# Attention probabilities scaled before their transposes on GpSimd, in place of scaling the product with the values

## The chip, the cores and the metric

The kernel runs on one core of a Trainium2 chip. The metric is the device time of one execution in microseconds (us); a lower one is better. The engines are named as the profile names them: PE is TensorE's matmul unit and PEld its weight load, DVE is VectorE, ACT is ScalarE, POOL is GpSimd, SP is SyncE, which issues the DMAs here.

## The reference

Two decoder layers over 512 tokens of width 1024. Each layer projects the normalised stream to two groups of attention heads: eight heads with a sliding window of 128 keys, two key heads and a learned sink, and eight heads with one key head, whose keys are chosen per query by an indexer (the best 128). Both groups go through one output projection; after it come a layer norm, a SwiGLU network of width 2816 with a gated input embedding, and another layer norm. What bears on the change is the softmax and the product with the values:

```python
# window group: the sink adds to the sum alone
m = jnp.maximum(s.max(-1, keepdims=True), sink)
pr = jnp.exp(s - m)
denom = pr.sum(-1, keepdims=True) + jnp.exp(sink - m)
o = jnp.einsum('bnhgqk,bnkhd->bnqhgd', (pr / denom).astype(v.dtype), vv)
...
# sparse group, over the chosen keys
pr = jax.nn.softmax(s, axis=-1)
o = jnp.einsum('bqhgj,bqjhd->bqhgd', pr.astype(v.dtype), vs)
```

All is float32.

## The kernel before

Tokens lie in four tiles of 128. Large products are made in three passes of a rounded format: each operand is split into a high half (a cast, on ACT) and a low half (what the cast lost, a subtract), and `mm3` (lines 325 to 327) multiplies high by high, high by low and low by high. The stream's own halves, turned so that features lie on partitions, are `fh` and `fl`; weight halves are in `wsp`, made by lines 278 (ACT) and 279 (POOL) of `w_split`, and by 256 and 257 for the down projection.

Attention is cut into 32 units, 16 a layer: a unit is one group of four heads on one tile of queries. Eight units of the window group come first ("a", with 128 keys for the first tile and 256 for the others), then eight of the sparse group ("b", with 128, 256, 384 and 512 keys, tile by tile). The sparse group computes all keys up to the query's tile and adds a mask that the top-k left in `work`.

A unit has two generators. `scores` multiplies queries by keys (L684), adds the mask and takes the row's extreme on DVE (L688), takes the exponential in place on ACT with the row's sum as a by-product (L692), adds the sink's share for the window group (L695 on POOL, L696 on ACT, L697 on POOL), and takes the reciprocal of the four sums on DVE (L698). The exponentials `es` are 128 queries by n keys for each head, not yet divided. L700 on POOL spreads the four reciprocals over `rb`, 128 x 256, 64 equal columns for each head.

`values` turns the exponentials on PE, 128 keys at a time, four heads to a bank (L721), copies them to SBUF on ACT (L723) and multiplies them with the values (`pv`, L715); two heads lie above each other on the 128 partitions of the product, so a product is 128 x 256. `rb` is turned too (L732) and copied to SBUF (L735), so that the reciprocals lie as the product does. DVE multiplies product and reciprocals (L740), ACT casts the result to its high half (L747), and POOL subtracts for the low half (L748). For the window group the halves go to a tile of their own, `ma`; for the sparse group straight into `fh` and `fl`.

The order of the work is written by Python generators that `Order.run` takes in turn by the cost that each yields. In a layer three streams run side by side: `attention`, in which the scores of a unit run beside the values of the unit two before it (`AHEAD` = 2); `rest`, which projects the sparse group's queries, waits for all units of the window group and then makes that group's half of the output projection; and `topk`, 16 rounds of two DVE operations for each of three tiles (L659, L660, and L662 at the end). From the order written down and from its own estimate of durations, the framework then lays out each engine's queue when the program is made; each engine works through its queue in that order. Scratch tiles `t2k` come from a pool of 12, PSUM banks from a pool of 8, shared by all.

Of the kernel before, what the change touches and what calls it, by code (L numbers as in the profile page):

```python
# [10 lines left out]
F32 = mybir.dt.float32  # L11
# [4 lines left out]
OP = mybir.AluOpType  # L16
# [80 lines left out]
def hybrid_kernel(ctx: ExitStack, tc: tile.TileContext, x, p, positions, ln_in_g, ln_in_b, w_in,  # L97
# [3 lines left out]
    PE, V, A, G, SP = nc.tensor, nc.vector, nc.scalar, nc.gpsimd, nc.sync  # L101
# [6 lines left out]
    small = ctx.enter_context(tc.tile_pool(name="small", bufs=4))  # L108
# [4 lines left out]
    def bank(tag, bufs, dt=F32):  # L113
        return psum.tile([128, 512], dt, name="bank", tag="bank", bufs=8)

    def acc():
        return bank("acc", 4)

    def slot(dt=F32R):
        return slots.tile([128, 512], dt, name="slot", tag="slot")  # L120

    def t2k(dt=F32):
        return tmp.tile([128, 512], dt, name="t2k", tag="t2k")

    def sm(n, name):
        return small.tile([128, n], F32, name=name, tag=name)
# [20 lines left out]
    idf = const.tile([128, 128], F32, name="idf")  # L147
# [200 lines left out]
    def tok(t):  # L348
        return slice(t * 128, (t + 1) * 128)
# [198 lines left out]
    for l in range(L):  # L548
# [84 lines left out]
        def wait(*keys):  # L633
            while not all(k in ready for k in keys):
                yield None
# [30 lines left out]
        def scores(kind, t, g, st):  # L666
            if kind == "a":
                k0, nk, c = max(0, t - 1) * 128, (256 if t else 128), g
                mask = win if t else win[:, 128:]
                yield from wait((kind, t, g), *[("k", b) for b in range(max(2, t + 1))])  # L670
            else:
                k0, nk, c = 0, (t + 1) * 128, 2
                yield from wait((kind, t, g), *[("k", b) for b in range(max(2, t + 1))], *[("s", t)] * (t > 0))
                mask = work[t] if t else causal[:, S - 128:]
            nn = max(nk, 256)
            per = 512 // nn
            ng, sums = sm(4, "ng"), sm(4, "sums")
            es = []
            for j in range(4):
                if j % per == 0:  # L680
                    ps, e = bank("sc", 2), t2k()
                o = j % per * nn
                for s in range(2):
                    PE.matmul(ps[:, o:o + nn], qT[kind, t, g][:, j * 128:(j + 1) * 128], kT[c, s][:, k0:k0 + nn],  # L684
                              start=(s == 0), stop=(s == 1))
                es.append(e[:, o:o + nk])
                far = nsink[:, l, 4 * g + j:4 * g + j + 1] if kind == "a" else 3e38
                V.tensor_tensor_reduce(es[j], ps[:, o:o + nk], mask, -HD ** -0.5, far, op0=OP.add, op1=OP.min,  # L688
                                       accum_out=ng[:, j:j + 1])
                yield 0.44 * nn / 512  # L690
            for j in range(4):
                A.activation(es[j], es[j], AF.Exp, bias=ng[:, j:j + 1], scale=-1.0, accum_out=sums[:, j:j + 1])  # L692
            if kind == "a":
                ek = sm(4, "ek")
                G.tensor_tensor(ek, sink[:, l, 4 * g:4 * g + 4], ng, OP.add)  # L695
                A.activation(ek, ek, AF.Exp)  # L696
                G.tensor_tensor(sums, sums, ek, OP.add)  # L697
            V.reciprocal(sums, sums)  # L698
            rb = small.tile([128, 256], F32, name="rb", tag="rb", bufs=3)
            G.tensor_copy(rb.rearrange("p (j d) -> p j d", j=4), sums[:, :, None].to_broadcast([128, 4, 64]))  # L700
            st.extend([es, rb, k0 // 128, nk // 128])

        def values(kind, t, g, st):

            es, rb, b0, nb = st
            c = g if kind == "a" else 2
            o = acc()[:, :256].rearrange("p (a n) -> p a n", a=2)
            pts = {}
            lag, cost = LAG[kind], 0.45
            if kind == "b":  # L710
                yield from wait("x read")

            def pv(b):
                for u in range(2):
                    PE.matmul(o[u * 64:(u + 1) * 64], vt[b0 + b][:, c * 64:(c + 1) * 64], pts[b][:, u],  # L715
                              start=b == 0, stop=b == nb - 1)

            for b in range(nb):
                ps = bank("tp", 2)
                for j in range(4):  # L720
                    PE.transpose(ps[:, j * 128:(j + 1) * 128], es[j][:, b * 128:(b + 1) * 128], idf)  # L721
                pt = t2k()
                A.copy(pt, ps)  # L723
                pts[b] = pt.rearrange("p (a u n) -> p u a n", a=2, u=2)
                yield 0.44
                if b >= lag:
                    pv(b - lag)
                    yield cost

            pr = bank("tp", 2)  # L730
            for a in range(2):
                PE.transpose(pr[:, a * 128:(a + 1) * 128], rb[:, a * 128:(a + 1) * 128], idf)  # L732
            tt = t2k()
            rr, of = (tt[:, i * 256:(i + 1) * 256].rearrange("p (a n) -> p a n", a=2) for i in range(2))
            A.copy(rr, pr[:, :256].rearrange("p (a n) -> p a n", a=2))  # L735
            yield 0.44
            for b in range(max(0, nb - lag), nb):
                pv(b)
                yield cost
            V.tensor_tensor(of, o, rr, OP.mult)  # L740
            if kind == "a":
                m = ma[t, g] = slot().rearrange("p (s a n) -> p s a n", s=2, a=2)
                hi, lo = m[:, 0], m[:, 1]
            else:
                k = 4 + 2 * g
                hi, lo = fh[:, k:k + 2, tok(t)], fl[:, k:k + 2, tok(t)]
            A.copy(hi, of)  # L747
            G.tensor_tensor(lo, of, hi, OP.subtract)  # L748
            ready.add(("m" + kind, t, g))

        units = [("a", t, g) for g in range(2) for t in range(NT)] + [("b", t, g) for t in range(NT) for g in range(2)]
# [1 line left out]
        def attention():  # L753

            st = {}
            for i in range(len(units) + AHEAD):
                gs = []
                if i in FILL:
                    yield 0.0, FILL[i]
                if i < len(units):  # L760
                    st[i] = []
                    gs.append(scores(*units[i], st[i]))
                if i >= AHEAD:
                    gs.append(values(*units[i - AHEAD], st.pop(i - AHEAD)))
                while gs:
                    none = True
                    for g in list(gs):
                        try:
                            c = next(g)
                        except StopIteration:  # L770
                            gs.remove(g)
                            none = False
                            continue
                        if c is not None:
                            none = False
                            yield c
                    if none:
                        yield None
# [186 lines left out]
        for gi, fs in enumerate(GROUPS):  # L965
            hs = []
            for f in fs:
# [7 lines left out]
                if gi == 1 and f == fs[0]:  # L975
                    pT = {}
                    for k in range(2):
                        ps = bank("tp", 2)
                        for t in range(NT):
                            o = t % 2 * 256 + k * 128  # L980
# [12 lines left out]
            for h in range(2):  # L993
                ps = [acc() for _ in range(NT)]
                n = len(hs)
# [13 lines left out]
        for b in TAIL:  # L1009
            for h in range(2):  # L1010
# [18 lines left out]
                for i, t in enumerate(b):  # L1029
                    a = t2k()  # L1030
# [37 lines left out]
```

## Time and profile before

| | |
|---|---|
| median of 3 runs | 1251.89 us (1251.59 to 1252.14) |
| the profiled execution | 1251.81 us, its span 1249.7 us |
| granted TensorE clock, mean | 0.998 |
| attention, layer 1 | 98 to 206 us of the span, about |
| attention, layer 2 | 702 to 816 us of the span, about |

How rows are read. A window's row gives its length and then, for each engine, the time in which it was busy and the number of instructions. A group's row has line, engine, operation, the tile written and the tiles read, the shapes and the count, then the busy time and the mean of one in ns, then the idle time of the engine before these instructions and what ended it. A row of one line's durations has minimum, median and maximum in ns, then the first and last start in us. A row of the timeline has start and duration in us, and in brackets the idle time before it. A row of the waits has who waited for whom, us in total, times, and the longest. The chain is the work that ended last, followed backwards; its row gives lines' shares of the window asked for.

### The profile page before, as it was taken

What the parts mean: (1) busy time and instruction counts of PE and PEld (TensorE: products, weight loads), DVE (VectorE), ACT (ScalarE), POOL (GpSimd) and SP (SyncE); (2) the same over time, 40 slices, a digit from 0 to 9 for tenths busy, and PEclk for the clock granted to TensorE, in tenths of its full rate; (3) what the DMA queues carried; (4) which work ended last, traced back from release to release, by engine and by line L of the source; (5) the groups of instructions that cost most, each with busy time, mean ns of one, the idle gap of its engine ahead of it and who ended that gap; (6) DMA issues with size and microseconds to landing.
All of it is one profiled execution on the core that took longest, in us unless ns stands there. A gap on an engine that the chain in (4) does not pass through costs nothing.

```text
span 1249.7 us, 18006 instructions
## 1 busy us (share of the span) xinstructions
PE 1225.9 (98%) x6552; PEld 1029.9 (82%) x6552; DVE 765.2 (61%) x1678; ACT 576.4 (46%) x1193; POOL 682.9 (55%) x555
## 2 busy tenths in 40 slices
PE   7999999999999999999999999999999999999996
PEld 5998777988888888888899987689888888888885
DVE  7699954682727272726677998286555555555365
ACT  6577763442434343433337787534343333333331
POOL 6885532566566666663169754234757575757400
PEclk9999999999999999999999999999999999999999
DMA  5232311333232323034033203114323333321321
GB/s 177 78 92 85 95 42 35 119 118 118 85 118 84 118 85 118 18 118 140 2 89 114 101 21 117 52 54 149 99 87 105 97 105 99 103 83 52 101 84 50
DMA packets 89264, 112.74 MB, mean 90 GB/s; under 512 B 5460, under 2 KB 66132, under 8 KB 89176
## 3 DMA queue, kind: packets, MB, share of 16 engines
q1 hardware_dynamic: 88504, 111.58, 28.5%
q8 instruction: 51, 0.84, 0.3%
q14 instruction: 37, 0.30, 0.1%
q10 hardware_dynamic: 672, 0.03, 0.0%
HBM read 109.49 MB, written 2.10 MB: 89 GB/s over the span
## 4 chain that ended last, share of the span: by engine, by line
PE 82%; POOL 5%; DVE 3%; issue 3%; ACT 3%; DMA 3%; SPq 0%; DVEq 0%; ACTq 0%; POOLq 0%
PE bank L325 24%; PE bank L326 24%; PE bank L327 24%; PE bank L715 3%; PE bank L684 3%; PE bank L721 2%; POOL wsp L279 2%; DMA wst<-in_w_pg_dram 2%; POOL wsp L257 1%; PE bank L523 1%; PE bank L438 1%; PE bank L732 1%; ACT wsp L278 1%; DVE slot L273 1%; POOL slot L517 1%
## 5 line engine op out<-in xcount | busy, mean ns | idle before, releaser
L279 POOL TENSOR_TENSOR wsp<-wst,wsp 128x1024 fp32r<-128x1024 f32 (+2 forms) x148 | 351.3, 2389 | 244.4 <-ACT wsp L278 240.8
L326 PE MATMUL bank<-fl,wsp 128*128 128x512 f32 (+1 forms) x768 | 284.8, 372 | 0.4 <-DVE fl L441 0.4
L325 PE MATMUL bank<-fh,wsp 128*128 128x512 f32 (+1 forms) x768 | 283.6, 372 | 1.0 <-ACT fh L440 1.0
L327 PE MATMUL bank<-fh,wsp 128*128 128x512 f32 (+1 forms) x768 | 283.1, 371 | 0.0
L278 ACT CAST wsp<-wst 128x1024 fp32r<-128x1024 f32 (+2 forms) x148 | 151.6, 1033 | 166.4 <-PE bank L327 126.2
L325 PE MATMUL bank<-wsp,fh 128*128 128x256 f32 (+3 forms) x512 | 165.2, 326 | 3.6 <-DVE work L648 2.0
L874 DVE TENSOR_TENSOR t2k<-bank,t2k 128x512 f32<-128x512 f32 x44 | 30.4, 692 | 222.0 <-PE bank L327 222.0
L326 PEld LDWEIGHTS bank<-fl,wsp 128*128 128x128 f32 x768 | 144.6, 188 | 25.7 <-DVE fl L441 0.9
L325 PEld LDWEIGHTS bank<-fh,wsp 128*128 128x128 f32 x768 | 143.6, 188 | 26.8 <-ACT fh L440 1.9
L327 PEld LDWEIGHTS bank<-fh,wsp 128*128 128x128 f32 x768 | 144.6, 188 | 24.9
L327 PE MATMUL bank<-wsp,fl 128*128 128x256 f32 (+3 forms) x512 | 163.7, 322 | 1.4 <-DVE fl L441 0.8
L326 PE MATMUL bank<-wsp,fh 128*128 128x256 f32 (+3 forms) x512 | 164.7, 322 | 0.0
L257 POOL TENSOR_TENSOR wsp<-slot,wsp 128x512 fp32r<-128x512 f32 x100 | 141.6, 1442 | 29.0 <-ACT wsp L256 29.0
L325 PE MATMUL bank<-wsp,slot 128*128 128x512 f32 x392 | 153.8, 392 | 0.0
L326 PE MATMUL bank<-wsp,slot 128*128 128x512 f32 x392 | 152.7, 390 | 0.0
L327 PE MATMUL bank<-wsp,slot 128*128 128x512 f32 x392 | 148.4, 390 | 0.0
L790 DVE TENSOR_TENSOR x<-bank,x 128x512 f32<-128x512 f32 x140 | 91.5, 684 | 88.5 <-PE bank L327 88.5
L904 ACT CAST slot<-t2k 128x256 fp32r<-128x256 f32 (+1 forms) x104 | 49.8, 497 | 144.1 <-DVE t2k L874 102.5
L257 POOL TENSOR_TENSOR wsp<-t2k,wsp 128x512 fp32r<-128x512 f32 x40 | 57.5, 1448 | 92.4 <-ACT wsp L256 92.4
L325 PEld LDWEIGHTS bank<-wsp,fh 128*128 128x128 f32 x512 | 97.6, 191 | 11.9 <-ACT fh L440 2.4
L327 PEld LDWEIGHTS bank<-wsp,fl 128*128 128x128 f32 x512 | 97.5, 191 | 7.9 <-DVE fl L441 1.1
L326 PEld LDWEIGHTS bank<-wsp,fh 128*128 128x128 f32 x512 | 98.0, 191 | 6.5 <-issue 1.2
(152 smaller groups left out, 2004.6 us busy)
## 6 DMA issues: line engine op xcount, KB each, us to landing
wst<-in_w_gu_dram SPq DMA_DIRECT2D x88, 512.0 KB, 3.5
slot<-in_w_down_dram SPq DMA_DIRECT2D x80, 256.0 KB, 2.8
wst<-in_w_in_dram SPq DMA_DIRECT2D x16, 512.0 KB, 3.6
wst<-in_w_o_dram SPq DMA_DIRECT2D x16, 512.0 KB, 3.8
wst<-in_w_pg_dram SPq DMA_DIRECT2D x16, 512.0 KB, 4.2
wst<-in_w_in_dram SPq DMA_DIRECT2D x8, 256.0 KB, 2.7
lng<-in_ln_g_dram SPq DMA_DIRECT2D x4, 512.0 KB, 4.8
lnb<-in_ln_b_dram SPq DMA_DIRECT2D x4, 512.0 KB, 5.5
```

The costliest lines, as they stand in the source:

```text
L257: G.tensor_tensor(w[:, 1, j], src[j], w[:, 0, j], OP.subtract)
L278: A.copy(w[:, 0, :a * n], st[:, :a * n])
L279: G.tensor_tensor(w[:, 1, :a * n], st[:, :a * n], w[:, 0, :a * n], OP.subtract)
L325: PE.matmul(o, sh, mh, start=start, stop=False, skip_group_check=again)
L326: PE.matmul(o, sh, ml, start=False, stop=False, skip_group_check=again)
L327: PE.matmul(o, sl, mh, start=False, stop=stop, skip_group_check=again)
L684: PE.matmul(ps[:, o:o + nn], qT[kind, t, g][:, j * 128:(j + 1) * 128], kT[c, s][:, k0:k0 + nn], start=(s == 0), stop=(s == 1))
L715: PE.matmul(o[u * 64:(u + 1) * 64], vt[b0 + b][:, c * 64:(c + 1) * 64], pts[b][:, u], start=b == 0, stop=b == nb - 1)
L721: PE.transpose(ps[:, j * 128:(j + 1) * 128], es[j][:, b * 128:(b + 1) * 128], idf)
L790: V.tensor_tensor(xt[t][:, c], ps, xt[t][:, c], OP.add)
L874: V.tensor_tensor(a, ps[1, f], a, OP.mult)
L904: A.copy(h[0], src)
```

## The change

`scores` no longer makes `rb`. Instead POOL multiplies each head's exponentials in place by the head's reciprocal, four instructions of 128 x n, each with a column of 128 numbers as the factor. `values` transposes these probabilities, so the product with the values needs no factor afterwards: the two transposes of `rb`, their PSUM bank, the copy, the scratch tile and the multiplication on DVE go. ACT casts the high half straight from the product in PSUM, and the low half's subtract moves from POOL to DVE, also reading PSUM. The step in the middle of `values` yields a cost of 0.22 instead of 0.44.

```diff
             V.reciprocal(sums, sums)
-            rb = small.tile([128, 256], F32, name="rb", tag="rb", bufs=3)
-            G.tensor_copy(rb.rearrange("p (j d) -> p j d", j=4), sums[:, :, None].to_broadcast([128, 4, 64]))
-            st.extend([es, rb, k0 // 128, nk // 128])
+            for j in range(4):
+                G.tensor_scalar(es[j], es[j], sums[:, j:j + 1], 1.0, op0=OP.mult, op1=OP.mult)
+            st.extend([es, k0 // 128, nk // 128])
 
         def values(kind, t, g, st):
 
-            es, rb, b0, nb = st
+            es, b0, nb = st
...
-            pr = bank("tp", 2)
-            for a in range(2):
-                PE.transpose(pr[:, a * 128:(a + 1) * 128], rb[:, a * 128:(a + 1) * 128], idf)
-            tt = t2k()
-            rr, of = (tt[:, i * 256:(i + 1) * 256].rearrange("p (a n) -> p a n", a=2) for i in range(2))
-            A.copy(rr, pr[:, :256].rearrange("p (a n) -> p a n", a=2))
-            yield 0.44
+            yield 0.22
             for b in range(max(0, nb - lag), nb):
                 pv(b)
                 yield cost
-            V.tensor_tensor(of, o, rr, OP.mult)
...
-            A.copy(hi, of)
-            G.tensor_tensor(lo, of, hi, OP.subtract)
+            A.copy(hi, o)
+            V.tensor_tensor(lo, o, hi, OP.subtract)
             ready.add(("m" + kind, t, g))
```

## The prediction

> **What bounds the kernel now.** I read the page's busy shares first, then the busy time of the engines in the four stretches in which attention runs, then the chain that ended last inside these stretches.
>
> ```profile
> span 1249.7 us, 18006 instructions
> PE 1225.9 (98%) x6552; PEld 1029.9 (82%) x6552; DVE 765.2 (61%) x1678; ACT 576.4 (46%) x1193; POOL 682.9 (55%) x555
> ```
> ```profile
> core 0: us, PE busy (x) PEld busy (x) DVE busy (x) ACT busy (x) POOL busy (x), PEclk, DMA share, GB/s
> 85.40:165.00 79.60, 78.81 (x589) 66.89 (x589) 73.47 (x245) 61.52 (x183) 45.61 (x66) 1.00 0.26 80
> 165.00:206.00 41.00, 41.00 (x238) 28.41 (x238) 13.52 (x40) 23.11 (x57) 13.47 (x14) 1.00 0.17 52
> 698.00:760.00 62.00, 61.08 (x476) 52.53 (x475) 59.31 (x196) 47.29 (x149) 38.31 (x59) 1.00 0.27 90
> 760.00:816.00 56.00, 55.75 (x327) 40.16 (x326) 27.41 (x86) 34.90 (x89) 18.11 (x19) 1.00 0.17 53
> ```
>
> In each layer attention has a first part (sliding-window units and the first sparse ones, rows one and three) and a second (sparse units over 384 and 512 keys, rows two and four). PE is full in all four. In the first part DVE is nearly full too (73.47 of 79.60, 59.31 of 62.00), since the rounds of top-k run there; in the second part PE is alone. The granted clock is 1.00 throughout. The chain inside both attention spans names PE's lines almost alone:
>
> ```profile
> by line: PE bank L715 17.9%; PE bank L684 15.7%; PE bank L721 14.5%; PE bank L325 14.4%; PE bank L327 13.8%; PE bank L326 13.7%; PE bank L732 3.8%; PE bank L523 2.7%; DVE t2k L688 0.7%; ACT t2k L723 0.5%; DVE work L660 0.5%; ACT slot L524 0
> by line: PE bank L715 16.0%; PE bank L684 15.7%; PE bank L325 14.6%; PE bank L326 14.2%; PE bank L327 13.9%; PE bank L721 11.8%; PE bank L732 3.7%; PE bank L523 2.8%; ACT t2k L723 2.4%; ACT t2k L692 2.2%; issue 1.2%; ACT slot L524 0.8%; ACT
> ```
>
> The first is of 98 to 206 us, the second of 702 to 816 us. L732, the pair of transposes that turns the rows of reciprocals, has 3.8% of 108 us and 3.7% of 114 us: 4.1 + 4.2 = 8.3 us of PE time on the path. That is the most that taking it away can return directly.
>
> **The change part by part.** A unit is one group of four heads on one block of 128 queries; there are 16 in a layer, 32 in all. Prices of what goes and what comes:
>
> ```profile
> L732 PE MATMUL bank<-idf,rb x64: 270/272/329, 103.6 to 808.5; 128*128 128x128 f32 x64
> 103.72 0.22 PE bank L732 x2
> 108.97 0.37 PE bank L732 x2
> L735 ACT COPY t2k<-bank 128x256 f32<-128x256 f32 x32 | 11.8, 369 | 9.3 <-PE bank L732 9.2
> L740 DVE TENSOR_TENSOR t2k<-bank,t2k 128x256 f32<-128x256 f32 x32 | 13.4, 419 | 28.7 <-PE bank L715 20.3 <-ACT t2k L723 8.3
> L747 ACT CAST fh<-t2k 128x256 fp32r<-128x256 f32 x16 | 6.6, 411 | 18.0 <-DVE t2k L740 17.8
> L511 DVE TENSOR_TENSOR t2k<-bank,tab 128x256 f32<-128x256 f32 x20 | 7.8, 415 | 0.0
> L700 POOL COPY rb<-sums 128x256 f32<-128x256 f32 x32 | 12.8, 403 | 35.6 <-DVE sums L698 35.6
> L748 POOL TENSOR_TENSOR fl<-t2k,fh 128x256 fp32r<-128x256 f32 x16 | 11.8, 740 | 38.7 <-ACT fh L747 36.4 <-DVE ng L688 2.2
> L748 POOL TENSOR_TENSOR slot<-t2k,slot 128x256 fp32r<-128x256 f32 x16 | 11.8, 737 | 5.1 <-ACT slot L747 4.8
> L491 POOL TENSOR_SCALAR tab<-t2k 128x128 f32<-128x128 f32 x1 | 0.3, 303 | 0.5 <-ACT t2k L481 0.5
> L491 POOL TENSOR_SCALAR tab<-t2k 128x64 f32<-128x64 f32 x1 | 0.2, 243 | 0.0
> L463 POOL TENSOR_SCALAR t2k<-t2k 128x192 f32<-128x192 f32 x2 | 1.7, 862 | 0.2
> L257 POOL TENSOR_TENSOR wsp<-slot,wsp 128x512 fp32r<-128x512 f32 x100 | 141.6, 1442 | 29.0 <-ACT wsp L256 29.0
> ```
>
> PE, removed: 64 transposes, in pairs. The chain gives a pair 0.22 us, or 0.37 where it follows L715; the 0.15 more is the end of L715's matmuls, which the next instruction will then wait for. So 32 x 0.22 = 7.0 us, on the path: **-7.0**. The ends are 0 (hidden, see the rivals) and 8.3.
>
> ACT, removed: 32 copies of 369 ns, 11.8 us. ACT is 77% busy at most (61.52 of 79.60), so they count only where PE waits for ACT. One such place is seen in layer 2:
>
> ```profile
> 778.59 0.38 ACT L735 COPY t2k<-bank 128x256 f32<-128x256 f32 x1
> 780.69 0.65 PE L715 MATMUL bank<-t2k,slot 128*64 128x256 f32 x4 [0.22 <-ACT t2k L723]
> ```
>
> The copy stands on ACT in front of what PE waits for. Its 0.38 us less is worth some 0.3 there: **-0.3** (ends 0 and 1). The cast to the high half (L747) reads PSUM instead of SBUF; L735, the same size from PSUM, is 369 against 411 ns: nothing.
>
> DVE: the multiplication goes (419 ns), the low half comes from POOL (L748). A DVE subtract from PSUM of that size costs about L511's 415 ns. Difference 32 x 4 ns: **0**. But it now waits for the cast, 0.4 us after the product, and what stands behind it on DVE (scores' masks L688, top-k) waits with it. This replaces L740's own wait for the product, and the result is ready 0.74 us sooner than over POOL; I take nothing, and at most 32 x 0.4 = 13 us of DVE time in the wrong direction if DVE's queue never had other work ahead.
>
> POOL: two operations go, 0.403 + 0.74 us a unit. Four multiplications of 128 x n come (n = 128, 256, 384 or 512 keys). No row shows POOL multiplying by a column of numbers. L491 is a multiply by constants: 243 ns at 64 columns and 303 at 128, so 0.94 ns a column on top of 183 ns: 424 ns at 256, 663 at 512. L463, subtract and multiply, takes 862 ns at 192: 3.54 ns a column on the same base, 1.09 us at 256. In between lies the two-input subtract, 740 ns at 256 and 1442 at 512. I take L491's, since the operation (two multiplications) is the same. The first part of layer 1 has twelve units: eight of the window, 2 x (4 x 0.303 + 12 x 0.424) = 12.6 us, two sparse ones over 128 keys, 2.4, and two over 256, 3.4; together 18.4 for 13.7 removed (12 x 1.14). POOL goes from 45.6 to 50.3 us of 79.6 and stays off the path. In its queue the weight halves (L279) and the rotary sums (L513, L517) stand behind the multiplications, 1.2 to 2.7 us in place of 0.4, but no longer behind L748 and its wait for the cast.
>
> By the Trainium skill, page "GPSIMD Engine Reference", section 4.1, a one-input operation on this engine runs at roughly line rate and only two-input ones are about twice as slow; L491 agrees (0.94 ns a column), L463 does not: it has one input and is slower than the two-input rows. By the page alone the multiplication would be of the cheap kind, and the sum is the one below.
>
> The new wait is the question. Now only the turned reciprocals wait for L698 and L700; the transposes of the probabilities (L721) wait for the exponentials. Afterwards they wait for the sums, the reciprocal and four multiplications. How late that is:
>
> ```profile
> 98.92 0.60 PE L721 MATMUL bank<-idf,t2k 128*128 128x128 f32 x4
> 98.98 0.17 DVE L698 RECIPROCAL sums<-sums 128x4 f32<-128x4 f32 x1
> 138.82 0.60 PE L721 MATMUL bank<-idf,t2k 128*128 128x128 f32 x4
> 142.47 0.16 DVE L698 RECIPROCAL sums<-sums 128x4 f32<-128x4 f32 x1
> 142.70 0.40 POOL L700 COPY rb<-sums 128x256 f32<-128x256 f32 x1 [0.38 <-DVE sums L698]
> 798.19 0.40 POOL L700 COPY rb<-sums 128x256 f32<-128x256 f32 x1 [4.00 <-DVE sums L698]
> 804.00 0.27 PE L721 MATMUL bank<-idf,t2k 128*128 128x128 f32 x1
> ```
>
> First unit: reciprocal over at 99.15, 0.3 us to POOL's start, four times 0.303: ready at 100.7, 1.7 us after its transposes run now. The worst (last window unit of layer 1): 142.63 + 0.3 + 1.7 = 144.6 against 138.82, 5.8 us. The last: 798.19 + 4 x 0.663 = 800.8 against 804.0, 3 us to spare. Worked out so for all 32, 14 units are late, by 38 us together, nearly all in the first parts. If PE stood still for it the change would cost 31 us; but PE's order is laid out anew when the program is made, and other work stands in front of what is late:
>
> ```profile
> PE bank L684 <- ACT slot L524: 0.6, 1, 0.6
> ```
>
> This is PE's only listed wait in 98 to 206 us, though every unit already passes through DVE, ACT and back. What is left is places without other work. The end of the window units is one:
>
> ```profile
> 138.89 2.39 POOL L279 TENSOR_TENSOR wsp<-wst,wsp 128x1024 fp32r<-128x1024 f32 x1 [0.70 <-ACT wsp L278]
> 142.05 0.50 PE L684 MATMUL bank<-slot 128*128 128x256 f32 x2 [0.59 <-ACT slot L524]
> 144.65 0.40 PE L325 MATMUL bank<-wsp,slot 128*128 128x512 f32 x1
> ```
>
> Query projections are over by then; the output projection begins at 144.65, and its weights are split on POOL until 141.28. The late unit's eight transposes (8 x 0.11 = 0.87 us) leave this stretch before other work can come in, and the 0.59 us of idle time may come once more: between 0.87 and 1.46, I take 1.15 a layer, **+2.3**. Bounds of the whole wait: 0, and 38.
>
> Order: the step without work now yields 0.22 instead of 0.44, so attention runs 16 x 0.22 = 3.5 us ahead of the projections in the order written down. No weights or DMAs are moved past it; I price it at nothing, since PE is full on both sides.
>
> Sum: -7.0 - 0.3 + 2.3 = -5.0. The profiled execution took 1251.81 us (span 1249.7 and 2.1 around it), the median of the runs is 1251.89, no different. Forecast: **1246.8 us**. No change that can be told is within 0.2%, 1249.4 to 1254.4.
>
> **The rivals.**
>
> *DVE holds the first parts, and PE's time there is hidden.* For it: DVE's 92% and 96% busy. Against: PE is 99% busy there as well, and the projections can move forward. Then only pairs of the second parts count, about six units a layer, 12 x 0.22 = 2.6 us, less the 2.3 of the new hole: 1251.5. Chance 0.14.
>
> *The wait takes the place of what is removed.* If 7 of the 38 us find no other work: 1251.8. For it: 14 late units in 140 us. Against: the single wait of PE above. Chance 0.12. A form of it is a lock between DVE and POOL:
>
> ```profile
> L662 DVE TENSOR_SCALAR work<-work x6: 352/428/1905, 87.9 to 771.9; 128x256 f32<-128x256 f32 x2, 128x384 f32<-128x384 f32 x2, 128x512 f32<-128x512 f32 x2
> ```
>
> This DVE step varies from 352 to 1905 ns without its size explaining it. If six of them stood behind one more multiplication of 0.66 us, DVE would lose 4 us, and of the gain 1 would be left (1250.8). The Trainium skill, page "SBUF — State Buffer", section "Who interferes with whom", says that the second port pair is an exclusive lock between POOL and such a step; the row's spread agrees. It is part of this chance.
>
> *POOL becomes the bound, slower.* At L463's price the twelve units of the first part cost 45.0 us: POOL's 45.6 become 76.9 of 79.6, and with waits for reciprocals (below, in 98 to 206 us) 93.
>
> ```profile
> POOL rb L700 <- DVE sums L698: 16.4, 7, 5.7
> ```
>
> That is 13.7 us over, a layer: 1251.8 - 7.3 + 27 = 1271. It decides from about 2.2 ns a column: at the two-input price it is 31.0 us, 62.9 + 16.4 = 79.3, just full. For it: no row shows the operation, and L463. Against: L491. Chance 0.12. With cheap multiplications, holes of over 10 us (1254.5 to 1262) have 0.07.
>
> *More than I take.* All 8.3 us, ACT's 1 and no hole: 1242.5. Chance 0.05.
>
> **How the numbers follow.** Forecast (1244 to 1249.3) 0.50; the two cases of no change 0.26; slower 0.19; more 0.05. Faster 0.55, the same 0.26, slower 0.19. The range runs from 1242.5 to 1257: it leaves out the dear multiplication and a little of the holes, some 0.15. The likeliest case's own range is 1244 to 1249.3.
>
> **What would show it.** Right: L732 and L735 gone, PE's busy time some 7 us less, four POOL rows of about 0.42 us at 256 columns, L721 behind them with little idle time on PE. The POOL price decides first: over 0.74 us at 256 columns the third rival is on. Idle PE in front of L721 released by POOL is the second. PE idle in the first parts, released by DVE, is the first. The forecast is wrong most easily through the new order of PE's queue, which no row of before shows.

## The result and the profile after

The changed kernel takes 1269.51 us in the median (1268.43 to 1269.81) against 1251.82 us for the kernel before on the same chip: a ratio of 1.0139, 95% interval [1.0127, 1.0151]. It is 17.7 us slower; 5.0 us faster were forecast, and the time lies above the range.

The busy shares of the changed kernel:

```profile
span 1266.6 us, 17932 instructions
PE 1226.3 (97%) x6488; PEld 1024.0 (81%) x6488; DVE 766.1 (60%) x1678; ACT 568.6 (45%) x1161; POOL 709.0 (56%) x619
```

64 transposes are gone (6552 to 6488), and PE's busy time is not a microsecond less. The span is 16.9 us longer, so PE stands idle where it did not before. Where, is read from windows cut at the stages' ends: attention of a layer from its first scores to the first residual of its output projection, the network between them, and the stretch from the end of layer 1's network to the scores of layer 2. Before:

```profile
core 0: us, PE busy (x) PEld busy (x) DVE busy (x) ACT busy (x) POOL busy (x), PEclk, DMA share, GB/s
90.00:202.60 112.60, 111.81 (x768) 88.47 (x767) 81.30 (x272) 80.39 (x232) 54.79 (x76) 1.00 0.24 76
202.60:583.20 380.60, 379.90 (x1785) 318.00 (x1784) 206.55 (x308) 143.67 (x221) 220.82 (x121) 1.00 0.31 97
583.20:700.00 116.80, 114.78 (x721) 105.09 (x721) 83.96 (x226) 56.86 (x127) 60.62 (x67) 1.00 0.26 75
700.00:812.80 112.80, 111.62 (x770) 88.64 (x769) 83.61 (x275) 80.63 (x233) 55.28 (x76) 1.00 0.23 75
```

The same windows after:

```profile
89.70:208.10 118.40, 111.14 (x737) 84.98 (x736) 82.43 (x271) 76.61 (x217) 68.54 (x109) 1.00 0.22 68
208.10:588.70 380.60, 379.90 (x1785) 317.97 (x1785) 206.35 (x308) 143.57 (x220) 220.05 (x120) 1.00 0.31 98
588.70:710.20 121.50, 116.63 (x723) 106.81 (x722) 84.83 (x229) 57.11 (x128) 60.91 (x68) 0.99 0.26 72
710.20:829.70 119.50, 111.38 (x737) 84.95 (x736) 82.90 (x273) 76.39 (x217) 68.93 (x109) 1.00 0.20 67
```

Attention is 5.8 and 6.7 us longer, the start of layer 2 4.7, the network nothing: 17.2 together. In attention PE's idle time (length less busy) goes from 0.8 and 1.2 us to 7.3 and 8.1. POOL is busy 68.5 of 118.4 us, so it is not the bound. The multiplications themselves cost what the prediction took, or little more:

```profile
L700 POOL TENSOR_SCALAR t2k<-t2k,sums 128x256 f32<-128x256 f32 x64 | 29.8, 484 | 9.8 <-DVE sums L698 6.9 <-PE bank L523 1.4 <-PE bank L721 1.4
L700 POOL TENSOR_SCALAR t2k<-t2k,sums 128x128 f32<-128x128 f32 x32 | 11.5, 378 | 9.2 <-DVE sums L698 9.2
L700 POOL TENSOR_SCALAR t2k<-t2k,sums 128x512 f32<-128x512 f32 x16 | 10.8, 695 | 20.2 <-DVE sums L698 20.2
L700 POOL TENSOR_SCALAR t2k<-t2k,sums 128x384 f32<-128x384 f32 x16 | 9.1, 590 | 8.4 <-DVE sums L698 8.4
```

What PE waits for is read at the two lines on either side of the change: the transposes of the probabilities (L721) and the products with the values (L715). Each row has idle time in front of the line, weight loads and matmuls added together, so a stop can stand in it twice. Before, L721 and then L715:

```profile
its engine sat idle before it (us, times) until:
  issue: 7.3, 19
```
```profile
  issue: 5.8, 25
  ACT t2k L723: 3.0, 9
```

After, L721 and then L715:

```profile
  POOL t2k L700: 11.5, 26
  issue: 6.2, 16
```
```profile
  ACT t2k L723: 21.9, 34
  issue: 5.3, 18
```

Two waits are new or have grown: transposes behind the multiplications, and products behind the copies of the transposes. The second was not in the prediction at all. The chain shows it in attention of layer 1 (98 to 212 us), where PE's lines no longer stand alone:

```profile
by line: PE bank L325 11.3%; PE bank L326 11.2%; PE bank L327 11.0%; PE bank L715 10.7%; DVE t2k L688 10.0%; PE bank L721 9.1%; PE bank L684 9.0%; DVE work L660 4.8%; DVE m L659 4.3%; POOL t2k L700 4.2%; issue 2.9%; POOL wsp L279 2.1%; ACT 
```

DVE's masks and top-k rounds (L688, L659, L660) now have 19.1% of the chain: masks stand in front of the exponentials and their sums, and a transpose now starts behind these.

The start of layer 2 has nothing to do with probabilities. The chain there, and two windows around its end:

```profile
672.39 4.43 DMA wst<-in_w_in_dram
...
676.90 1.04 ACT wsp L278
677.94 0.38 ACT bank L647
678.32 0.70 ACT slot L613 x4
```
```profile
675.60:679.00 3.40, 0.34 (x1) 0.08 (x1) 1.44 (x5) 2.10 (x7) 3.26 (x3) 1.00 0.68 184
679.00:683.00 4.00, 3.94 (x21) 3.94 (x22) 3.54 (x12) 2.22 (x12) 2.92 (x4) 0.62 0.69 203
```

In ACT's queue, a cast that PE needs (L613) stands behind a weight cast (L278) that waits for its DMA. PE stops for 3.1 us, and then the granted clock is 0.62 for 4 us.

### The profile page after: what moved, and what is told of

Same layout as the page of the kernel before. It is cut to its first block, busy times and chain, and to the rows that moved or that the text cites. A ratio compares the mean times of both kernels' runs of the same rounds, so it can differ in the third digit from the quotient of the medians.

```text
span 1266.6 us, 17932 instructions
## 1 busy us (share of the span) xinstructions
PE 1226.3 (97%) x6488; PEld 1024.0 (81%) x6488; DVE 766.1 (60%) x1678; ACT 568.6 (45%) x1161; POOL 709.0 (56%) x619
## 4 chain that ended last, share of the span: by engine, by line
PE 82%; DVE 5%; POOL 4%; ACT 3%; issue 2%; DMA 2%; SPq 0%; ACTq 0%; DVEq 0%; POOLq 0%
PE bank L325 25%; PE bank L326 25%; PE bank L327 25%; PE bank L715 2%; PE bank L684 2%; PE bank L721 2%; POOL wsp L279 2%; DVE t2k L688 1%; DMA wst<-in_w_pg_dram 1%; POOL slot L517 1%; POOL t2k L700 1%; PE bank L438 1%; PE bank L523 1%; ACT wsp L278 1%; DVE slot L273 1%
## 5 line engine op out<-in xcount | busy, mean ns | idle before, releaser
L279 POOL TENSOR_TENSOR wsp<-wst,wsp 128x1024 fp32r<-128x1024 f32 (+2 forms) x148 | 351.2, 2387 | 261.8 <-ACT wsp L278 260.7
L278 ACT CAST wsp<-wst 128x1024 fp32r<-128x1024 f32 (+2 forms) x148 | 151.6, 1033 | 174.1 <-PE bank L327 134.1
```

The source lines that it names most:

```text
L278: A.copy(w[:, 0, :a * n], st[:, :a * n])
L279: G.tensor_tensor(w[:, 1, :a * n], st[:, :a * n], w[:, 0, :a * n], OP.subtract)
```

## The experiments

Totals are medians, ratios are against the kernel before on the same chip. Edits are against the changed kernel, if nothing else is said. Lengths of stages are of the profiled executions, cut as above.

One caution holds for all of them. The start of layer 2 moves by itself: before the change it takes 116.8 us, in the changed kernel 121.5, and in the runs below 116.2 to 119.5, with and without multiplications. In some of the longer ones PE has no stop as in the changed kernel, but the granted clock is 0.50 for 3.4 us there (in the run with ones from the rotary table, 669.8 to 673.2 us). So a difference of 2 to 3 us between totals can come from there; where it does, attention is given beside the total.

### Is it POOL's work or the wait?

**No multiplications.**

```diff
-            for j in range(4):
-                G.tensor_scalar(es[j], es[j], sums[:, j:j + 1], 1.0, op0=OP.mult, op1=OP.mult)
```

> The changed kernel without its four multiplications a unit: it leaves out the division by the sum, and the transposes wait for the exponentials alone, as before the change. Theory W (the transposes now wait for sums, reciprocal and multiplication) and theory P (the multiplications load POOL) both expect the forecast's gain: 1245 to 1248 us, with attention's first layer about 4 us shorter than before the change. Theory O (it is the moved subtract on DVE, or the new order of the queues in itself) expects 1260 or more.

1250.25 us, ratio 0.9988 [0.9979, 0.9997]. Without division the rest of the change gives 1.5 us, not 7. The time lies above what theories W and P expected, and far below theory O's.

**The multiplications without the wait.** First with a tile of ones made for it:

```diff
+    one = const.tile([128, 1], F32, name="one")
+    G.memset(one, 1.0)
...
-                G.tensor_scalar(es[j], es[j], sums[:, j:j + 1], 1.0, op0=OP.mult, op1=OP.mult)
+                G.tensor_scalar(es[j], es[j], one, 1.0, op0=OP.mult, op1=OP.mult)
```

> The changed kernel with the multiplications' factor taken from a column of ones that is made at the start: POOL's work is the same, but nothing waits for the sums and the reciprocal any more (the division is left out). Theory W, if the wait for the reciprocal is what costs: 1248 to 1255 us. Theory P, if the multiplications' own time on POOL costs: 1265 to 1270, as the changed kernel.

1265.59 us, 1.0112 [1.0097, 1.0127], but not because of attention, which is 110.8 and 112.4 us long: the network is 387.4 us instead of 380.6. The largest group of dense products is slower there, in each of its three passes. The row of one of the passes, in this kernel and in the kernel before:

```profile
L326 PE MATMUL bank<-fl,wsp 128*128 128x512 f32 x640 | 253.1, 396 | 0.0
```
```profile
L326 PE MATMUL bank<-fl,wsp 128*128 128x512 f32 x640 | 249.0, 389 | 0.0
```

The new small tile takes room in SBUF; that other tiles then lie elsewhere is a likely cause, which was not tried by itself. So the run was made again with ones that lie there already, the first column of the rotary frequencies:

```diff
-                G.tensor_scalar(es[j], es[j], sums[:, j:j + 1], 1.0, op0=OP.mult, op1=OP.mult)
+                G.tensor_scalar(es[j], es[j], invf[:, 0:1], 1.0, op0=OP.mult, op1=OP.mult)
```

> As e2_const, but the column of ones is the first column of a table that the kernel has anyway (the inverse frequencies, 1.0 in its first column), so no tile moves in SBUF; the division is left out. In e2_const the matmuls of the dense network themselves took longer (0.232 to 0.235 us apart in place of 0.227), which has nothing to do with waits. Theory W (the reciprocal's wait): attention 111 to 113 us a layer as without multiplications, the whole 1249 to 1254 us. Theory P (the multiplications' own time on POOL): attention 117 to 120 us, the whole 1262 or more.

1252.68 us, 1.0004 [0.9995, 1.0014]; network 380.7 us, attention 111.3 and 112.9, as without multiplications (112.1 and 112.8). POOL's work is all there and costs attention nothing; the 2.4 us more in the total are at the start of layer 2 (119.0 against 116.2). The waits at L721 and L715, which were 11.5 and 21.9 us in the changed kernel:

```profile
  POOL t2k L700: 1.5, 4
```
```profile
  ACT t2k L723: 9.9, 18
```

Against this run the changed kernel differs only in where the factor comes from, and in the queues laid out for it: 1269.51 - 1252.68 = 16.8 us. Attention has 13.7 of them, the price of waiting on the reciprocal; the start of layer 2 has 2.5.

**The wait with less work:** only one column in 128 is multiplied.

```diff
+                ec = es[j].rearrange("p (b n) -> p b n", n=128)[:, :, 0:1]
-                G.tensor_scalar(es[j], es[j], sums[:, j:j + 1], 1.0, op0=OP.mult, op1=OP.mult)
+                G.tensor_scalar(ec, ec, sums[:, j:j + 1], 1.0, op0=OP.mult, op1=OP.mult)
```

> The changed kernel with each multiplication cut to one column in 128: the transposes still wait for the reciprocal and for POOL, but POOL's work falls from some 0.4 to 0.7 us an instruction to about 0.2 (the division is left out for the other columns). Theory W: 1262 to 1268 us, close to the changed kernel. Theory P: 1248 to 1255.

1260.93 us, 1.0075 [1.006, 1.009], just below what theory W expected and above theory P. An instruction on two columns still took 271 ns, so POOL's work is about half (32.0 of 61.2 us) and the loss against no multiplications 10.7 us. The other half of the work, which costs nothing where the factor is ready, costs 8.6 us more behind the reciprocal. Some 4 of those lie at the start of layer 2 (121.5 against 117.7).

**The work without the wait of the transposes,** in the kernel before: the same columns multiplied (in two halves where a head has over 256 keys), into `rb`, ahead of the copy of the reciprocals.

```diff
+            w = nk if nk <= 256 else nk // 2
+            for j in range(4):
+                for c0 in range(0, nk, w):
+                    G.tensor_scalar(rb[:, :w], es[j][:, c0:c0 + w], sums[:, j:j + 1], 1.0, op0=OP.mult, op1=OP.mult)
             G.tensor_copy(rb.rearrange("p (j d) -> p j d", j=4), sums[:, :, None].to_broadcast([128, 4, 64]))
```

> The kernel before the change, with the same multiplications on POOL added, their result written to the tile of spread reciprocals and overwritten by it: POOL's load without any new wait for the transposes (the turned reciprocals alone wait longer). Theory W: 1252 to 1256 us. Theory P: 1262 or more.

1280.21 us, 1.0236 [1.0219, 1.0253]: the expectation that POOL's work is free there, 1252 to 1256, failed. The transposes of the reciprocals in this kernel:

```profile
  POOL rb L704: 33.3, 15
```

The copy of the reciprocals (L704) stands behind the multiplications, and PE waits for it. Theory P's 1262 or more came by this wait, not by load: the run does not isolate POOL's load, as it was meant to. It shows again that such work is dear between a reciprocal and its reader.

### Where did the gain from the pair go?

**No division, with a pair of transposes that nobody reads:**

```diff
+            pr = bank("tp", 2)
+            for a in range(2):
+                PE.transpose(pr[:, a * 128:(a + 1) * 128], idf, idf)
             yield 0.22
```

> The changed kernel without multiplications (e1_no_mult, 1250.25 us), with a pair of transposes of the identity put back at the old place, written to a bank that nothing reads (the division is left out). If the pair covers the wait of the last product for the last copy of turned probabilities, as the starts of PE's instructions suggest, taking it away was worth nothing: 1249 to 1252 us, as with and without it. If PE's time for the pair lies on the path, as the forecast had it, 1256 to 1258.

1255.68 us, 1.0032 [1.002, 1.0043]: 5.4 us more than without the pair, just under the forecast's range. The pair does lie on the path; something else in the change takes its gain back.

**The kernel before, with the low half's subtract on DVE:**

```diff
-            G.tensor_tensor(lo, of, hi, OP.subtract)
+            V.tensor_tensor(lo, of, hi, OP.subtract)
```

> The kernel before the change with one part of it: the subtract for the low half moves from POOL to DVE (reading SBUF). Theories W and P: no effect or a small gain, since POOL is relieved of 0.74 us a unit and of its wait for the cast: 1249 to 1253 us. Theory O (the moved subtract holds DVE up): 1256 or more.

1252.77 us, 1.0008 [0.9999, 1.0017]: 0.8 us slower, at most 2.1 by the interval, too little for theory O.

**The written step,** 0.22 in place of 0.44, alone in the kernel before:

```diff
-            yield 0.44
+            yield 0.22
```

> The kernel before, with the step behind the pair of transposes written as 0.22 in place of 0.44. Theory O: the products come before their copies here too; the wait grows from 3.0 us to 6 to 10 and the time is 1255 to 1259. Rival P: the pair still lies between, nothing moves, 1251 to 1253.

1258.80 us, 1.0059 [1.0044, 1.0074]: 7.0 us slower, and all of it in attention (117.3 and 115.7 us). At L715:

```profile
  ACT t2k L723: 11.9, 15
```

3.0 us were there before. The step decides how much work of the projections is written between a unit's last transposes and its last products. With less, PE comes to the products before ACT has copied the transposes. The pair, still there, does not cover it.

**No division, the step written as 0.44:** 

> The changed kernel without the division (as in the run without multiplications), with the step between the last transposes and the last products with the values written as 0.44 again in place of 0.22. The run without multiplications gave back only 1.6 us of the pair's 7, and there the products with the values wait 11.8 us (16 times) for the copies of the transposed probabilities, where before they waited 3.0 us (9 times). Theory O (the order written down: with nothing between the last transposes and the last products, the products come before their copies, and the pair's gain is lost there): the wait falls to 3 to 7 us and the time to 1243 to 1247. Rival P (the pair itself was the cover, as matmuls on PE, and a written step without work moves nothing): the wait stays at 10 to 13 us and the time at 1249.5 to 1251.5.

1248.12 us, 0.9969 [0.9958, 0.9981], just above the expected range; the products wait 3.9 us for their copies, as expected. Attention is 110.5 and 109.8 us, 4.6 less than with 0.22, while the start of layer 2 grew by 2.8 us (119.0).

**No division, the step written as 0.88:** 

> The same without the division, the step written as 0.88. Theory O: the wait of the products for the copies is 3 us or less and the time 1242.5 to 1246. Rival P: the wait stays near 12 us and the time at 1249.5 to 1251.5. A third way, that the step delays the whole chain of attention behind the projections: 1252 to 1258.

1242.62 us, 0.9927 [0.9913, 0.9942]. Attention is 107.6 and 108.4 us long and PE never stops, as its window for layer 1 shows:

```profile
89.40:197.00 107.60, 107.52 (x737) 85.43 (x736) 81.57 (x272) 76.32 (x217) 38.29 (x45) 1.00 0.24 79
```

**The kernel before, the step written as 0.88:** 

> The kernel before, with the written step of 0.88 in place of 0.44. From 0.22 to 0.44 it gained 7.0 us, with the products' wait for their copies going from 11.9 to 3.0 us. Theory O: at most the 3.0 us that are left go, 1248.5 to 1251. If the step is at its best already: 1251 to 1253. If the chain of attention ends later by it: 1254 to 1258.

1252.44 us, 1.0004 [0.9995, 1.0014]. With the pair there is nothing more to be had from the step.

So at equal steps taking the pair, its copy and the two operations away, without dividing, is worth 1258.80 - 1250.25 = 8.6 us (0.22), 3.7 (0.44; before 1251.8) and 9.8 (0.88). In attention alone it is 8.1, 5.2 and 9.6 us. The 7.0 of the step itself had hidden it.

### Do the two waits add?

**The changed kernel, the step written as 0.44:** 

> The changed kernel with the step written as 0.44 again. There the products with the values wait 21.9 us (34 times) for the copies of the transposed probabilities. Theory O: some 5 us of that go, 1263 to 1266. Theory W alone (all of the loss is the transposes' wait for the reciprocal and the paced multiplications, which are as late as before): 1268 to 1271. The layer-2 start, 4.6 us longer in the changed kernel by the order of ACT's queue, may fall back by itself, so the time is to be read without it.

1268.41 us, 1.0134 [1.0117, 1.0151], close to the changed kernel, but by two differences that cancel: attention is 5.0 us longer (119.2 and 123.7 us), the start of layer 2 4.7 us shorter (116.8). The products' wait fell from 21.9 to 8.7 us, and that of the transposes rose:

```profile
  POOL t2k L700: 22.9, 15
```

Most of it is one stop in each layer (4.46 and 4.72 us; the row above counts it for weight loads and for matmuls), at the place that the prediction named, the end of the window units. The timeline of layer 1, and three windows:

```profile
140.29 2.36 POOL L279 TENSOR_TENSOR wsp<-wst,wsp 128x1024 fp32r<-128x1024 f32 x1 [1.09 <-ACT wsp L278]
...
142.60 0.21 POOL L697 TENSOR_TENSOR sums<-sums,ek 128x4 f32<-128x4 f32 x1
...
143.00 3.24 POOL L700 TENSOR_SCALAR t2k<-t2k,sums 128x128 f32<-128x128 f32 x8 [0.19 <-DVE sums L698]
...
143.53 0.17 DVE L698 RECIPROCAL sums<-sums 128x4 f32<-128x4 f32 x1
...
144.93 0.69 PE L721 MATMUL bank<-idf,t2k 128*128 128x128 f32 x2 [4.46 <-POOL t2k L700]
```
```profile
140.00:145.00 5.00, 0.54 (x5) 0.08 (x4) 4.93 (x15) 1.74 (x9) 4.51 (x8) 0.70 0.35 97
145.00:149.00 4.00, 3.91 (x22) 3.32 (x22) 3.67 (x10) 2.32 (x5) 1.25 (x3) 0.52 0.99 346
149.00:152.00 3.00, 3.00 (x18) 2.44 (x15) 2.97 (x9) 0.94 (x5) 0.98 (x2) 1.00 0.21 79
```

For the last window unit, a weight half on POOL (L279) stands in front of the sum (L697), the sum in front of the reciprocal (143.53), the reciprocal in front of the multiplications. Of the eight in the row of L700, which names the shape of the first alone, these are the last four, from 144.40 us on: the first four belong to the first sparse unit, whose reciprocal needs no sum from POOL, and stand ahead in the queue. PE waits 4.46 us, and for the next 4 us the granted clock is 0.52; by an estimate that loses some 1.9 us more (4 x 0.48). Theory O's range is missed, and theory W's is met by accident: read without the start of layer 2, as the expectation says, the step costs some 4 us.

**The changed kernel, the step written as 0.88:** 

> The changed kernel with the written step of 0.88 in place of 0.22. Without the division this step brought 7.6 us (1250.2 to 1242.6). Theory S (the two waits are separate: products behind their copies, and transposes behind reciprocal and multiplications; the step takes only the first away): 1260 to 1263. Rival M (PE is short of other work as long as the transposes are late, so one wait only moves into the other, as it did with 0.44: products' wait 21.9 to 8.7 us, transposes' wait 11.5 to 22.9): 1266 to 1271.

1268.69 us, 1.0134 [1.0119, 1.0149]. As the rival expected, one wait moves into the other: that of the products falls from 21.9 to 14.9 us, that of the transposes rises from 11.5 to 15.6, and attention is 1.2 us longer.

**Ones as the factor, the step written as 0.88:** 

> The multiplications by a column of ones that is there from the start (no wait for the reciprocals, the division left out), with the step of 0.88. If POOL's multiplications by themselves are free even where PE has no waits left: 1242 to 1245, as without them. If they cost (on POOL's queue, or with DVE): 1248 to 1253.

1244.05 us, 0.9935 [0.9918, 0.9951], 1.4 us above the run without multiplications. So even with PE full, more than 60 us of work on POOL cost no more than that, and attention is not longer for it (107.3 and 107.7 us). The reciprocal's wait alone is the difference of 24.6 us to the run above, 24.1 of them in attention.

### Distance

**Scores three units ahead of the values,** in the changed kernel:

```diff
-D_GI, D_KI, D_K, D_Q, AHEAD = 9.0, 13.0, 8.0, 10.0, 2
+D_GI, D_KI, D_K, D_Q, AHEAD = 9.0, 13.0, 8.0, 10.0, 3
```

> The changed kernel with the values of a unit written down three units behind its scores instead of two, so that sums, reciprocal and multiplications have one unit more before the transposes need them. Theory W (lateness of the scaled probabilities): attention comes back to 111 to 114 us a layer, the whole 1250 to 1258 us, unless the 12 scratch tiles run short (two to four a unit are held one unit longer). Theory P (load on POOL): no change, 1266 to 1272.

1260.85 us, 1.0072 [1.0057, 1.0087]: neither expectation. The transposes' wait for POOL falls from 11.5 to 3.2 us. But scores, which now come earlier, wait 15.3 us for their queries (L524; two stops of 4.55 and 2.75 us), so attention is 118.8 and 115.8 us, only 3.3 less than in the changed kernel; 4.0 more come from the start of layer 2.

**Distance three and the step 0.88:** 

> The changed kernel with scores three units ahead of the values in place of two, and the step of 0.88. Theory S, and M too, since the transposes wait only 3.2 us in all at this distance: the step's 7.6 us come back, 1252 to 1255. A third way, that the longer attention keeps the queries' copies on ACT late and PE short of other work: 1258 to 1261, no gain over the distance alone (1260.9).

1248.33 us, 0.9972 [0.9961, 0.9984]: faster than both kernels, and than any of the expectations. Attention is 109.0 and 110.7 us, 18.2 less than in the changed kernel. At L721 and at L715:

```profile
  POOL t2k L700: 1.7, 5
```
```profile
  ACT t2k L723: 8.1, 15
```

**The kernel before with both:** 

> The kernel before, with scores three units ahead of the values and the step of 0.88. With both, the changed kernel took 1248.3 us, 3.4 less than before. If that gain is the pair's (its 7 us of PE time, now that neither wait is in the way): here 1251 to 1255, no gain. If it belongs to distance and step, and the change has no part in it: 1243 to 1249.

1250.92 us, 0.9991 [0.9982, 1.0]. So of the 3.4 us some 1 belongs to the distances, and the rest is 2.4 us by the two ratios (0.9991 - 0.9972), whose intervals just overlap. By stages the change gains 3.8 us in attention (219.7 against 223.5 for both layers). The start of layer 2 is 2.6 us shorter in the changed form and the dense parts 2.7 us longer, for reasons that were not traced; the two cancel.

**The kernel before with distance three alone:** 

> The kernel before, with the distance of three alone. The changed kernel gained 8.7 us by the distance, because its transposes no longer waited for the multiplications. Before, the transposes wait for nothing of that kind, so theory W gives no gain: 1251 to 1256 (the queries' copies come under more pressure, as in the changed kernel with that distance). If the distance is good in itself: 1243 to 1249.

1270.95 us, 1.0153 [1.0136, 1.017]: neither expectation. Attention is 120.4 and 121.5 us long. One stop stands out in each layer, and in layer 1 its consequences in the window behind it:

```profile
144.84 1.65 PE L684 MATMUL bank<-slot 128*128 128x256 f32 x6 [4.55 <-ACT slot L524]
...
764.54 1.65 PE L684 MATMUL bank<-slot 128*128 128x256 f32 x6 [3.69 <-ACT slot L524]
```
```profile
145.00:149.00 4.00, 4.00 (x20) 4.00 (x21) 3.90 (x14) 1.99 (x8) 0.93 (x2) 0.53 0.96 326
```

It is the same place as in the changed kernel with the step 0.44, for another reason: scores come to PE before their queries have been copied. So in these runs this place has no other work in reserve, whatever is late there.

## Why the prediction was wrong

The runs make a path from one kernel to the other. The last two columns split each step by stages of the profiled executions, whose times lie up to 1.2 us from the medians:

| step | us | from | attention, both layers | start of layer 2 |
|---|---|---|---|---|
| step written as 0.22 | +7.0 | 1251.8 to 1258.8 | +7.5 | +0.4 |
| pair, its copy and two operations away, subtract to DVE | -8.6 | to 1250.25 | -8.1 | -1.0 |
| multiplications, factor ready | +2.4 | to 1252.68 | -0.7 | +2.8 |
| factor is the reciprocal | +16.8 | to 1269.51 | +13.7 | +2.5 |

- **The new wait, taken as +2.3, is the step that failed.** It is worth 16.8 in the total, 13.7 in attention. The lateness was seen: 38 us for 14 units, the worst 5.8 us at the end of the window units of layer 1, where the step of 0.44 then shows a stop of 4.46 us. What was wrong is "other work stands in front of what is late". The argument was that PE had a single listed wait before, although each unit passes through three engines. But the runs fit an order that was free of waits because exponentials came early enough, not because PE had work in reserve. With probabilities later the reserve is short: the step of 0.44 takes 13 us of waiting from the products and gives 11 to the transposes, and a longer step brings attention down, while the reciprocal is waited for, only together with more distance (from 239.1 to 219.7 us in both layers at the step 0.88, the total from 1268.7 to 1248.3). The bound of 38 us stood in the working, and the range made little of it.
- **The order, priced at nothing, is the second failed step: +7.0.** "PE is full on both sides" was no reason. The step is the distance between a copy and its reader; the row to look at was the products' wait for the copies, 3.0 us, and what stood between. The prediction did name the new order of PE's queue as its weakest point, but gave it no price.
- **The pair and the copies, -7.3, were right in size,** though not exactly: 8.6 at the step 0.22, 9.8 at 0.88, and 3.7 at 0.44 (in attention 8.1, 9.6 and 5.2). The run without multiplications (1.5) would have said otherwise, had the step not been tried by itself.
- **The multiplications' price was right:** 484 ns at 256 columns against 424, 695 at 512 against 663, in place of L463's 1.09 us. From 128 to 512 columns the rows give (695 - 378)/384 = 0.83 ns a column. The Trainium skill, page "GPSIMD Engine Reference", section 4.1, puts one-input operations on this engine at roughly line rate and only two-input ones at about half the speed; these rows agree in that the multiplication is the cheaper (484 ns against 740 for the two-input subtract at 256 columns).
- **DVE at nothing** was right to about 0.8 us, which its interval (up to 2.1) does not tell from nothing. The lock between POOL and DVE that the second rival brought up can be worth little: multiplications without a wait cost 1.4 us with PE full, and nothing in attention.
- **Not seen:** the start of layer 2, 4.7 us. The stop there comes from ACT's order. The changed kernel with the step 0.44 or 0.88 does not show it (116.8 and 116.7 us), so it hangs on how the queues were laid out this time, not on probabilities. Which estimate tipped that order was not tried.
- **The rivals.** The third gave 1271 and would have been close for a wrong reason: POOL is at 58%. The right mechanism was the second rival, whose sign (idle PE in front of L721, released by POOL) came; its size was not its 1251.8, and lies even beyond the holes of 1254.5 to 1262 that had 0.07.

## What to carry to other kernels

When an operation moves from the end of a chain into its middle, count how late its reader becomes at each unit, and believe that other work will cover it only where the trace shows work that can move there; a full engine without waits is no proof of a reserve. A number in a schedule that changes along with the code is a change of its own: run it alone, in both forms. Distances between producer and reader work together: for the changed kernel a longer step alone gained nothing, a longer lead alone 8.7 us (3.3 in attention), both 21.2 (18.2 in attention); in the kernel before the lead alone cost 19 us. And split a difference of a few us by stages before it is given a cause: here a stage that had nothing to do with the change moved by up to 4.7 us.

## What was not expected of the hardware

- A stop of PE can cost more than its length. A stop of 0.96 us left the granted clock at 1.00 (the changed kernel, layer 1); after 3.1 us it was 0.62 for the next 4 us, after 4.5 us 0.52 and 0.53. Even a stop of 1.52 us was followed by 0.59, in the kernel before with the step of 0.22:

```profile
145.10:149.00 3.90, 3.85 (x14) 3.35 (x15) 3.87 (x14) 2.44 (x10) 1.49 (x3) 0.59 0.67 214
```

  The length does not decide alone: in layer 2 of the same run a stop of 1.52 us left the clock at 1.00 (760.9 to 764.9 us). What else decides was not tried.

  The Trainium skill, page "TensorE: Matmul & The Clock Gate", Part 1, says that the clock falls to half after an idle window of about 3.4 us and comes back after about as long a busy one. The depth and the way back agree with the traces (in the changed kernel with the step 0.44, the clock is 0.50 at 764 to 768 us behind the stop of 4.72 us; in layer 1 it is 1.00 again at 149 us, 4 us after PE went on); the length of stop that is enough does not: it is less than half of that here.
- With one more 128 x 1 tile in SBUF, 640 dense products of 128 x 512 in each of three passes took 396 ns in the mean against 389, and the time was 12.9 us longer (1265.59 against 1252.68). Whether it is the placement, and what about it, was not tried.
- A multiplication by a column on POOL took 271 ns even for two columns. Four of them, which overlap a little, put some 1.0 us between a reciprocal and the last of its readers:

```profile
109.77 0.98 POOL L701 TENSOR_SCALAR t2k<-t2k,sums 128x2 f32<-128x2 f32 x4 [0.94 <-DVE sums L698]
```
